# One kernel, three edits: the order of the two heads in probabilities-by-values, a transposed copy of the input from the host, and a contiguous layout for the compression operand

## The chip, the core and the metric

The program runs on one core of a Trainium2 chip. The metric is the device time of one execution in microseconds (us). TensorE (PE) does the matrix products, VectorE (DVE) and ScalarE (ACT) the elementwise work, GpSimd (POOL) a little of it, and SyncE (SP) issues most of the DMAs. PSUM is the memory that PE writes to, SBUF the one that it reads from.

## The reference, cut to what matters

One sequence of 512 tokens, 1024 wide, goes through four blocks. The parts that the change touches are these:

```
first block, layer 0:  gated delta rule (GDN)
    proj = x @ w_in                # x is the kernel's input; 4096 columns for q, k, v, z, and 16 for a and b
first block, layer 1:  native sparse attention (NSA)
    kc, vc = compress_blocks(...)  # 31 blocks of 32 tokens, one every 16 tokens:
        blk = x[:, 16*n + (0..31)] + pos          # n = 0..30
        silu(blk.reshape(31, 32*64) @ w1) @ w2
    per head: o = gate * (softmax(q k^T + bias) @ v), for the selected and the window branch
second block, two layers: per head, softmax(q k^T) @ v in the MLA branch and in the chunked branch
```

After each attention and GDN layer of the first block comes a mixture of experts (MoE), which the change leaves alone.

## The kernel before, in words

All operands of the large products are fp32 numbers split into two parts, hi and lo. `Net.split` (lines 107 and 108) copies the rounded value on ACT (line 107) and subtracts it on DVE (line 108). `Net.mm3` (lines 112 to 114) then makes three products, hi*hi, hi*lo and lo*hi, into the same PSUM tile. The activations that such a product needs stand in a pair `xh`, `xl` of eight tiles of 128 features by 512 tokens.

Weights come as chunks of 128x1024 (512 KB) through a ring of four SBUF buffers called `raw` (`Net.chunk`, DMA at line 96 on SP's queue). A buffer is free again when its chunk is split.

The kernel is written in a framework that puts the instructions of each engine in order before the run, by its own model of when each would be ready, with earlier work in program order first. An engine then runs its queue strictly in that order. A PE instruction whose operand is not ready holds back all that is behind it. Where the model saw a gap in front of an instruction, it has put a later one there that was ready.

**Start.** SP's queue loads the constants `call` (line 78), then the input `x` in four chunks of 128 tokens (line 1753, in `tile_network`), then small things of `gdn`: `row`, `nw`, `cw`, `wab` (lines 242 to 270). Each chunk of `x` is transposed on PE in eight pieces (`to_xt`, line 187) into PSUM and split from there. `wab` holds the 16 columns for a and b. It is split (`wabh`, `wabl`), and 24 products of `mm3` with 16 output rows follow, into a PSUM tile `br`. Then comes the projection of k with the first chunk of `g_w`.

**Compression.** `nsa` projects the keys and values to be compressed and stores them in `X0` and `X1`, tiles of 128x5x512. Partitions 0 to 63 hold the features of token t, partitions 64 to 127 those of token t+1, so that one product takes two of a block's 32 tokens. `x_evac` fills them from PSUM (lines 130 and 132, 16 copies of 64 partitions by 512 or 511). `compress` (line 1210) then makes 16 products for each of k and v. The moving operand is `Xs[i][:, :, l:l + 481:16]`: five groups (four heads and the position embedding) of 31 elements, 16 elements apart, 155 columns in all.

**Probabilities by values.** `softmax_t` works on one head: for each of four query tiles scores, a maximum with the bias (line 1142), the exponential (1144), its scaling on DVE (1147 or 1149), transposes on PE (187), and copies to `PT` on ACT (1151). Two heads u = 0 and 1 share a PSUM tile `o`, head 0 in partitions 0 to 63 and head 1 in 64 to 127, so each product uses half of PE's columns. The products (line 1333 in `nsa`, line 1613 in `pv_pair` of the second block) run over four key tiles jt, with 512, 384, 256 and 128 columns, and within each over u = 0, 1. Each fp32 product stands as two instructions in the trace, so a pair of heads has 16. There are 16 such pairs in NSA (four groups, two pairs of heads, two branches) and 16 in the second block (two layers, two branches, four pairs).

Around them stand products that are ready early and have no other hurry: the queries of the next group in NSA, and the gate and branch projections (PSUM tile `br`) in the second block.

Of the kernel before, what the change touches and what calls it, by code (L numbers as in the profile page):

```python
# [19 lines left out]
T = 512  # L20
# [45 lines left out]
class Net:  # L66
    def __init__(self, ctx, tc, I, out, dbg):
        self.tc, self.nc, self.I, self.out, self.dbg = tc, tc.nc, I, out, dbg
        self.cst = ctx.enter_context(tc.tile_pool(name="cst", bufs=1))
        self.ring = ctx.enter_context(tc.tile_pool(name="ring", bufs=1))  # L70
        self.big = ctx.enter_context(tc.tile_pool(name="big", bufs=1))
        self.lnp = ctx.enter_context(tc.tile_pool(name="lnp", bufs=1))
        self.ps, self.banks, self.pool = None, {}, ExitStack()
        self.dr = ctx.enter_context(tc.tile_pool(name="dr", bufs=1, space=bass.MemoryType.DRAM))
        nc = self.nc
        names, arr = _consts()
        call = self.cst.tile([128, arr.shape[1]], F32, name="call")
        nc.sync.dma_start(call, I["cst"])
        self.c = {n: call[:, j * 128:(j + 1) * 128] for j, n in enumerate(names)}
        self.ident = self.c["ident"]  # L80
        self.pows = self.cst.tile([128, 32], F32, name="pows")
        nc.vector.memset(self.pows, -0.5)
        self.flip = self.turn = self.turn2 = 0
        self.more, self.pairs = [], []


    def dump(self, name, ap):
# [140 lines left out]

def gdn(net, xt, aside):

# [4 lines left out]
    with ExitStack() as cx:  # L235
# [28 lines left out]
        with ExitStack() as c1:  # L264
# [3 lines left out]
            nc.sync.dma_start(cw, I["g_cw"])  # L268
            wab = p1.tile([128, 128], F32, name="wab")
            nc.sync.dma_start(wab, I["g_ab"])  # L270
            wabh = p1.tile([128, 128], F32R, name="wabh")
            wabl = p1.tile([128, 128], F32R, name="wabl")
            net.split(wabh, wabl, wab)
            XN = p1.tile([128, 32, 64], F32, name="XN")
# [806 lines left out]
def _prep_nsa(i, a):  # L1081
# [14 lines left out]
    a["n_w2"] = np.concatenate([w2[0], w2[0], w2[1]], 1)  # L1096
    a["n_pos"] = np.concatenate(ps, 1)
    a["n_rel"] = i["rel_bias"].T
# [61 lines left out]
def nsa(net, xt):  # L1160
# [4 lines left out]
    with ExitStack() as cx:  # L1165
# [11 lines left out]
        with ExitStack() as c1:  # L1177
# [10 lines left out]
            for i in range(2):  # L1188
                X = p1.tile([128, 5, T], F32, name=f"X{i}")
                G.memset(X[:, 4], 0.0)  # L1190
                G.memset(X[64:128, :, T - 1:], 0.0)
                G.dma_start(X[:, 4, 0:32], I["n_pos"][:, i * 32:i * 32 + 32])
                Xs.append(X)
            def x_evac(m, ps):
                X = Xs[m // 2]
                for j in range(2):
                    s = slice(j * 64, j * 64 + 64)
                    net.copy(X[0:64, 2 * (m % 2) + j], ps[s])
                    net.copy(X[64:128, 2 * (m % 2) + j, :T - 1], ps[s, 1:])
            net.proj_t([w[j] for j in range(4)], xh, xl, x_evac)  # L1200

            def compress(i):
                hp = net.psum()
                hv = hp[:, :155].rearrange("p (g n) -> p g n", n=31)
                for c in range(2):
                    raw = net.ring.tile([128, RING], F32, name="raw", tag="raw", bufs=RAW)
                    nc.sync.dma_start(raw, I["n_w1"][2 * i + c])
                    for k in range(8):
                        l = 2 * (c * 8 + k)
                        PE.matmul(hv, lhsT=raw[:, k * 128:k * 128 + 128], rhs=Xs[i][:, :, l:l + 481:16],  # L1210
                                  start=l == 0, stop=l == 30)
                hb = p1.tile([128, 2], F32, name="hb", tag="hb", bufs=2)
# [41 lines left out]
        with ExitStack() as c2:  # L1254
# [17 lines left out]
            for g in range(4):  # L1272
# [41 lines left out]
                for pr in range(2):  # L1314
# [5 lines left out]
                    for br in range(2):  # L1320
# [10 lines left out]
                        for jt in range(NT):  # L1331
                            for u in range(2):
                                PE.matmul(o[u * 64:u * 64 + 64, jt * 128:],  # L1333
                                          lhsT=vv[:, jt, br * 256 + g * 64:br * 256 + g * 64 + 64],
                                          rhs=pt_rhs(PTs[u], jt), start=False, stop=br == 1 and jt == NT - 1)
# [53 lines left out]
class Second:  # L1389
# [27 lines left out]
    def run(self, done, aside=lambda: None):  # L1417
# [6 lines left out]
        with ExitStack() as cx:  # L1424
# [180 lines left out]
            with ExitStack() as c2:  # L1605
                ap = c2.enter_context(tc.tile_pool(name="att", bufs=1))

                def pv_pair(PTs, vt, p, i, yf):
                    o = net.psum()
                    for jt in range(NT):  # L1610
                        for u_ in range(2):
                            h = 2 * p + u_
                            PE.matmul(o[u_ * 64:u_ * 64 + 64, jt * 128:], lhsT=vt[:, jt, h * 64:h * 64 + 64],  # L1613
                                      rhs=pt_rhs(PTs[u_], jt), start=jt == 0, stop=jt == NT - 1)
# [118 lines left out]
def tile_network(ctx: ExitStack, tc: tile.TileContext, I, out, dbg=()):  # L1733
# [16 lines left out]
    net.phase(mm=4, tp=2, br=2)  # L1750
    for t in range(NT):
        xx = net.ring.tile([128, RING], F32, name="raw", tag="raw", bufs=RAW)
        nc.sync.dma_start(xx, tiles(x)(t))
        net.to_xt(xx, t, *xt, tag="mm")
    moe_setup(net)
    y = gdn(net, xt, lambda room: bias_setup(net, room))
    xt = []

# [24 lines left out]
def _arrays(inputs):  # L1783
    i = {k: np.asarray(v) for k, v in inputs.items()}
    a = {"x": i["x"][0], "cst": _consts()[1], "cm": _consts_moe(), "cb": _consts_bf(), "rope": _rope_tables()}
    for prep in (_prep_gdn, _prep_moe, _prep_nsa, _prep_second):
# [18 lines left out]
```

## Time and profile before

| what | us |
|---|---|
| median of 3 runs | 2218.19 (2217.37 to 2220.05) |
| the profiled execution's own time | 2215.26 |
| span of the profile, first to last instruction | 2213.5 |
| PE busy in the span | 2114.8 (96%) |
| PE weight loads busy | 1683.9 (76%) |
| DVE busy | 1436.8 (65%) |
| ACT busy | 1122.9 (51%) |
| POOL busy | 363.0 (16%) |

Busy time of PE is from the start of an instruction to its modelled end. Back-to-back matmuls overlap, so the distance from one start to the next tells what one costs. A timeline row that stands for n instructions alike gives the time from the first's start to the last's end. In brackets stands how long the engine had been idle before, and what released it.

### The profile page before, as it was taken

The page shows a single profiled execution, that of the slowest core. Times are in us where ns is not written, and L with a number is a line of the kernel's source. Part 1 is how long each engine was busy: PE and PEld are TensorE (multiplying, and loading weights), DVE is VectorE, ACT ScalarE, POOL GpSimd, SP SyncE. Part 2 cuts the span into 40 slices and gives each one's busy share as a digit, 9 for nine tenths or more (in the row PEclk, how much of TensorE's full clock was granted, in tenths as well). Part 3 has the DMA queues.
Part 4 walks back from the last instruction along what each step waited for, and adds up shares of the span by engine and source line. Part 5 has one row for each costly group of instructions (what it writes and reads, how often), then busy time and mean ns, then how long its engine had stood idle before and what let it go on. Part 6 is the DMA issues. An engine that isn't in the chain of part 4 may idle for free.

```text
span 2213.5 us, 30328 instructions
## 1 busy us (share of the span) xinstructions
PE 2114.8 (96%) x10689; PEld 1683.9 (76%) x10689; DVE 1436.8 (65%) x2902; ACT 1122.9 (51%) x2238; POOL 363.0 (16%) x367
## 2 busy tenths in 40 slices
PE   8998988999999989899989999999999999999998
PEld 6777876877877656688778877787877887777786
DVE  6787666899538876689965554554456556455544
ACT  4545542987337776298743334544344324445432
POOL 4411013553100001355320010000011001000000
PEclk9999997999999999799999999999999999999999
DMA  6344536998441102699856555333435646433442
GB/s 205 95 133 122 163 132 241 338 329 281 139 123 49 48 29 94 232 355 334 286 161 199 157 154 156 119 105 136 150 110 171 205 134 176 133 114 110 143 152 76
DMA packets 133805, 364.86 MB, mean 165 GB/s; under 512 B 28544, under 2 KB 41296, under 8 KB 131856
## 3 DMA queue, kind: packets, MB, share of 16 engines
q1 hardware_dynamic: 80448, 271.65, 36.8%
q0 software_dynamic: 19744, 54.62, 7.9%
q10 hardware_dynamic: 33456, 36.59, 5.5%
q8 instruction: 86, 1.41, 0.3%
q14 instruction: 71, 0.58, 0.1%
HBM read 314.17 MB, written 64.61 MB: 171 GB/s over the span
## 4 chain that ended last, share of the span: by engine, by line
PE 65%; DVE 5%; DMA 5%; issue 4%; ACT 3%; POOL 1%; DVEq 0%; POOLq 0%; ACTq 0%; SPq 0%
PE mm L112 10%; PE mm L114 10%; PE mm L113 9%; PE br L113 6%; PE br L112 6%; PE br L114 5%; PE tp L187 5%; PE mm L966 5%; PE mm L1333 2%; PE mm L1613 2%; DMA xh<-in_m_w_dram 2%; DMA raw<-in_m_w_dram 1%; ACT hi L107 1%; DVE lo L108 1%; PE mm L1327 1%
## 5 line engine op out<-in xcount | busy, mean ns | idle before, releaser
L108 DVE TENSOR_TENSOR lo<-raw,hi 128x1024 fp32r<-128x1024 f32 x266 | 339.1, 1278 | 305.5 <-ACT hi L107 303.6
L107 ACT CAST hi<-raw 128x1024 fp32r<-128x1024 f32 x276 | 288.5, 1047 | 431.3 <-PE br L113 149.8
L112 PE MATMUL mm<-xh,hi 128*128 128x512 f32 x688 | 273.1, 397 | 1.7 <-DVE acc L316 1.7
L113 PE MATMUL mm<-xl,hi 128*128 128x512 f32 x688 | 271.1, 394 | 0.0
L114 PE MATMUL mm<-xh,lo 128*128 128x512 f32 x688 | 270.5, 394 | 0.1
L112 PE MATMUL mm<-hi,xh 128*128 128x512 f32 (+1 forms) x480 | 189.3, 394 | 4.9 <-ACT xh L107 4.1
L114 PE MATMUL mm<-hi,xl 128*128 128x512 f32 (+1 forms) x480 | 188.7, 394 | 1.1 <-DVE xl L108 1.0
L113 PE MATMUL mm<-lo,xh 128*128 128x512 f32 (+1 forms) x480 | 188.0, 392 | 0.0
L112 PE MATMUL br<-xh,hi 128*128 128x512 f32 x464 | 184.7, 398 | 2.2 <-DVE tm L1598 1.9
L113 PE MATMUL br<-xl,hi 128*128 128x512 f32 x464 | 186.6, 402 | 0.0
L114 PE MATMUL br<-xh,lo 128*128 128x512 f32 x464 | 182.7, 394 | 0.0
L1144 ACT ACTIVATE s<-s,mx 128x128 f32<-128x128 f32 (+3 forms) x256 | 143.1, 561 | 21.5 <-DVE mx L1142 20.8
L112 PEld LDWEIGHTS mm<-xh,hi 128*128 128x128 f32 x688 | 130.9, 190 | 29.6 <-issue 2.4
L114 PEld LDWEIGHTS mm<-xh,lo 128*128 128x128 f32 x688 | 130.1, 189 | 28.3 <-DVE lo L108 1.2
L113 PEld LDWEIGHTS mm<-xl,hi 128*128 128x128 f32 x688 | 130.8, 190 | 26.8
L1151 ACT COPY PT<-tp 128x128 f32<-128x128 f32 (+3 forms) x256 | 103.0, 425 | 30.8 <-PE tp L187 29.7
L112 PEld LDWEIGHTS mm<-hi,xh 128*128 128x128 f32 x480 | 91.5, 191 | 24.7 <-ACT xh L107 5.6
L966 PE MATMUL mm<-hi,xeh 128*128 128x512 f32 x256 | 109.8, 429 | 0.0
L187 PE MATMUL tp<-call,s 128*128 128x128 f32 x640 | 107.8, 278 | 0.8 <-ACT PT L1151 0.4
L114 PEld LDWEIGHTS mm<-hi,xl 128*128 128x128 f32 x480 | 91.4, 190 | 21.1 <-DVE xl L108 3.2
L187 PEld LDWEIGHTS tp<-call,s 128*128 128x128 f32 x640 | 74.9, 140 | 41.6 <-ACT PT L1151 17.1
L113 PEld LDWEIGHTS mm<-lo,xh 128*128 128x128 f32 x480 | 91.4, 190 | 17.5 <-issue 0.2
(514 smaller groups left out, 4562.9 us busy)
## 6 DMA issues: line engine op xcount, KB each, us to landing
raw<-in_s_w_dram SPq DMA_DIRECT2D x128, 512.0 KB, 3.6
raw<-in_m_w_dram SPq DMA_DIRECT2D x48, 512.0 KB, 10.4
xh<-in_m_w_dram SPq DMA_DIRECT2D x44, 512.0 KB, 11.8
raw<-in_g_w_dram SPq DMA_DIRECT2D x40, 512.0 KB, 3.7
xl<-in_m_w_dram SPq DMA_DIRECT2D x40, 512.0 KB, 12.8
raw<-in_n_w_dram SPq DMA_DIRECT2D x32, 512.0 KB, 3.8
ho<-in_m_w_dram SPq DMA_DIRECT2D x24, 512.0 KB, 9.2
raw<-in_s_br_dram SPq DMA_DIRECT2D x24, 512.0 KB, 3.5
```

Of the source, the lines that this page charges most:

```text
L107: self.nc.scalar.copy(hi, src)
L108: (eng or self.nc.vector).tensor_tensor(lo, src, hi.bitcast(F32), op=OP.subtract)
L112: mm(ps, lhsT=ah, rhs=bh, start=start, stop=False)
L113: mm(ps, lhsT=ah, rhs=bl, start=False, stop=False)
L114: mm(ps, lhsT=al, rhs=bh, start=False, stop=stop)
L187: self.nc.tensor.transpose(tp[:, j], src(b + j), self.ident)
L966: PE.matmul(pg, lhsT=a[:, c * 2 + k], rhs=b[:, k * 512:k * 512 + 512], start=c + j == 0, stop=c == 3 and j == 5)
L1144: S.activation(p[:, :n], s[:, :n], AF.Exp, bias=mx, scale=-1.0, accum_out=sm)
L1151: S.copy(PT[:, t:4 * t + 1:3], tp)
L1327: PE.matmul(ps[:, :n], lhsT=qs[j][:, ts], rhs=kh[:, :n], start=True, stop=False)
L1333: PE.matmul(o[u * 64:u * 64 + 64, jt * 128:], lhsT=vv[:, jt, br * 256 + g * 64:br * 256 + g * 64 + 64], rhs=pt_rhs(PTs[u], jt), start=Fals ...
L1613: PE.matmul(o[u_ * 64:u_ * 64 + 64, jt * 128:], lhsT=vt[:, jt, h * 64:h * 64 + 64], rhs=pt_rhs(PTs[u_], jt), start=jt == 0, stop=jt == NT - 1)
```

## The change

Three edits.

1. The loop over the two heads in probabilities by values runs u = 1 first, then u = 0, at both places.
2. The host passes a second copy of the input, transposed (`xT`, eight pieces of 128 features by 512 tokens). The kernel loads two pieces at a time into a ring buffer and splits them straight into `xh`, `xl`; the transposes of `x` go. `wab` is loaded first of all, through a ring buffer, and split at once into a tile that shares its memory with a later one (tag `pg`). The constants are loaded after the input.
3. `X0` and `X1` become 128x5x8x32: element (k, n) is token 16n + 2k on partitions 0 to 63, and token 16n + 2k + 1 on 64 to 127. The copies out of PSUM take every second token into that order, 256 elements each, and the moving operand of a product is 31 elements side by side. The host lays out the position embedding alike, padded with zeros, and the memsets of `X` go.

```diff
@@ Net.__init__, Net.consts
-        nc.sync.dma_start(call, I["cst"])
+    def consts(self):
+        self.nc.sync.dma_start(self.call, self.I["cst"])
@@ new function
+def gdn_small(net):
+    ab = net.lnp.tile([128, D], F32R, name="pg", tag="pg", bufs=1)
+    wabh, wabl = ab[:, 0:128], ab[:, 128:256]
+    wab = net.ring.tile([128, RING], F32, name="raw", tag="raw", bufs=RAW)[:, :128]
+    net.nc.sync.dma_start(wab, net.I["g_ab"])
+    net.split(wabh, wabl, wab)
+    return wabh, wabl
@@ gdn
-            wab = p1.tile([128, 128], F32, name="wab")
-            nc.sync.dma_start(wab, I["g_ab"])
-            wabh = p1.tile([128, 128], F32R, name="wabh")
-            wabl = p1.tile([128, 128], F32R, name="wabl")
-            net.split(wabh, wabl, wab)
@@ _prep_nsa (host)
-    a["n_pos"] = np.concatenate(ps, 1)
+    ps = np.concatenate(ps, 1).reshape(128, 2, 2, 8, 2)[..., 0].transpose(0, 1, 3, 2)
+    a["n_pos"] = np.concatenate([ps, np.zeros((128, 2, 8, 30), ps.dtype)], 3).reshape(128, 512)
@@ nsa
-                X = p1.tile([128, 5, T], F32, name=f"X{i}")
-                G.memset(X[:, 4], 0.0)
-                G.memset(X[64:128, :, T - 1:], 0.0)
-                G.dma_start(X[:, 4, 0:32], I["n_pos"][:, i * 32:i * 32 + 32])
+                X = p1.tile([128, 5, 8, 32], F32, name=f"X{i}")
+                G.dma_start(X[:, 4].rearrange("p r n -> p (r n)"), I["n_pos"][:, i * 256:i * 256 + 256])
@@ x_evac
-                    s = slice(j * 64, j * 64 + 64)
-                    net.copy(X[0:64, 2 * (m % 2) + j], ps[s])
-                    net.copy(X[64:128, 2 * (m % 2) + j, :T - 1], ps[s, 1:])
+                    v = ps[j * 64:j * 64 + 64].rearrange("p (n r u) -> p u r n", r=8, u=2)
+                    for u in range(2):
+                        net.copy(X[u * 64:u * 64 + 64, 2 * (m % 2) + j], v[:, u])
@@ compress
-                        l = 2 * (c * 8 + k)
-                        PE.matmul(hv, lhsT=raw[:, k * 128:k * 128 + 128], rhs=Xs[i][:, :, l:l + 481:16],
-                                  start=l == 0, stop=l == 30)
+                        PE.matmul(hv, lhsT=raw[:, k * 128:k * 128 + 128], rhs=Xs[i][:, :, k, c:c + 31],
+                                  start=c + k == 0, stop=c == 1 and k == 7)
@@ nsa, line 1332, and pv_pair, line 1611
-                            for u in range(2):
+                            for u in (1, 0):
@@ tile_network
-    for t in range(NT):
+    g_small = gdn_small(net)
+    for j in range(4):
         xx = net.ring.tile([128, RING], F32, name="raw", tag="raw", bufs=RAW)
-        nc.sync.dma_start(xx, tiles(x)(t))
-        net.to_xt(xx, t, *xt, tag="mm")
+        for u in range(2):
+            nc.sync.dma_start(xx[:, u * T:u * T + T], I["xT"][2 * j + u])
+        v = xx.rearrange("p (k t) -> p k t", k=2)
+        net.split(xt[0][:, 2 * j:2 * j + 2], xt[1][:, 2 * j:2 * j + 2], v)
+    net.consts()
```

## Rows read from the trace of the kernel before

**Rows 1.** The page's part 4: the last chain, share of the span by engine.
```profile
PE 65%; DVE 5%; DMA 5%; issue 4%; ACT 3%; POOL 1%; DVEq 0%; POOLq 0%; ACTq 0%; SPq 0%
```

**Rows 2.** Busy time by stretch: PE, PEld, DVE, ACT, POOL; granted clock, DMA share, GB/s.
```profile
560.00:660.00 100.00, 98.71 (x461) 77.94 (x460) 42.97 (x77) 34.92 (x56) 8.73 (x16) 1.00 0.40 128
...
676.00:722.00 46.00, 45.93 (x260) 32.56 (x258) 39.26 (x149) 35.37 (x106) 0.00 (x0) 1.00 0.14 45
...
1310.00:1424.00 114.00, 113.83 (x565) 88.17 (x566) 58.09 (x169) 54.90 (x130) 0.46 (x4) 1.00 0.54 160
```

**Rows 3.** Timeline of the start: start, duration, engine, line, operation, count.
```profile
4.98 5.71 PE L187 MATMUL mm<-call,raw 128*128 128x128 f32 x32 [4.98 <-DMA raw<-in_x_dram]
...
6.95 4.09 SPq L96 DMA_DIRECT2D raw<-in_g_w_dram  x4
...
12.22 0.30 ACT L107 CAST wabh<-wab 128x128 fp32r<-128x128 f32 x1 [0.74 <-DMA wab<-in_g_ab_dram]
...
12.57 0.40 PE L112 MATMUL br<-xh,wabh 128*16 128x512 f32 x1 [1.89 <-ACT wabh L107]
...
13.43 1.05 ACT L107 CAST hi<-raw 128x1024 fp32r<-128x1024 f32 x1 [0.92 <-DMA raw<-in_g_w_dram]
...
14.51 3.72 DVE L108 TENSOR_TENSOR lo<-raw,hi 128x1024 fp32r<-128x1024 f32 x3 [1.61 <-ACT hi L107]
...
18.13 0.40 PE L112 MATMUL mm<-xh,hi 128*128 128x512 f32 x1
...
18.64 0.69 SPq L96 DMA_DIRECT2D pg<-in_m_w_dram  x1
```

**Rows 4.** Timeline of PE, the two compressions.
```profile
611.40 8.59 PE L1210 MATMUL mm<-X,raw 128*128 128x155 f32 x32
...
630.72 8.59 PE L1210 MATMUL mm<-X,raw 128*128 128x155 f32 x32
```

**Rows 5.** Timeline of PE in GDN: fp32 products with a contiguous moving operand.
```profile
301.23 1.06 PE L556 MATMUL mm<-vp,XT 128*128 128x128 f32 x8
```

**Rows 6.** Line 130's copies into X: count, then ns minimum, median, maximum.
```profile
L130 ACT COPY X<-mm x8: 581/583/586, 587.1 to 603.6; 64x512 f32<-64x512 f32 x8
```

**Rows 7.** Timeline of PE in the second block, MLA branch, and at its end.
```profile
1335.22 1.07 PE L1613 MATMUL mm<-PT,vt 128*64 128x512 f32 x2
1336.23 0.98 PE L187 MATMUL tp<-call,s 128*128 128x128 f32 x7
1336.96 0.48 PE L112 MATMUL br<-xh,hi 128*128 128x512 f32 x1
...
1338.08 2.37 PE L1613 MATMUL mm<-PT,vt 128*64 128x512 f32 x14
1340.37 0.50 PE L113 MATMUL br<-xl,hi 128*128 128x512 f32 x1
...
2077.24 1.07 PE L1613 MATMUL mm<-PT,vt 128*64 128x512 f32 x2
```

**Rows 8.** Timeline of PE in the second block, chunked branch.
```profile
1434.00 2.37 PE L1613 MATMUL mm<-PT,vt 128*64 128x512 f32 x16
1436.31 0.50 PE L112 MATMUL br<-xh,hi 128*128 128x512 f32 x1
```

**Rows 9.** Timeline of DVE beside the split at 1335.22.
```profile
1335.67 0.49 DVE L1147 TENSOR_SCALAR s<-s,sm 128x512 f32<-128x512 f32 x1
```

**Rows 10.** Timeline of all engines in NSA, the first pair.
```profile
681.80 1.07 PE L1333 MATMUL mm<-PT,vv 128*64 128x512 f32 x2
...
682.24 0.55 DVE L1149 TENSOR_SCALAR s<-s,sm,gt 128x512 f32<-128x512 f32 x1
...
682.81 0.55 PE L187 MATMUL tp<-call,s 128*128 128x128 f32 x3
```

**Rows 11.** Timeline of PE in NSA, between two groups of heads.
```profile
822.20 1.09 PE L187 MATMUL tp<-call,pc 128*128 128x128 f32 x4 [4.88 <-DVE pc L1310]
```

**Rows 12.** Busy time in that stretch, columns as in rows 2.
```profile
821.20:827.90 6.70, 5.03 (x14) 3.52 (x15) 1.89 (x7) 1.59 (x5) 0.00 (x0) 0.50 0.00 0
```

More of the change, by code (lines that the diff above doesn't have):

```diff
@@ L76, in __init__ @@
         names, arr = _consts()
-        call = self.cst.tile([128, arr.shape[1]], F32, name="call")
-        nc.sync.dma_start(call, I["cst"])
-        self.c = {n: call[:, j * 128:(j + 1) * 128] for j, n in enumerate(names)}
+        self.call = self.cst.tile([128, arr.shape[1]], F32, name="call")
+        self.c = {n: self.call[:, j * 128:(j + 1) * 128] for j, n in enumerate(names)}
         self.ident = self.c["ident"]
@@ L226, in rows, with gdn @@
         return r
-def gdn(net, xt, aside):
+def gdn_small(net):
[5 more added lines that the diff above has]
+    return wabh, wabl
+def gdn(net, xt, aside, wabh, wabl):
     tc, nc, I = net.tc, net.nc, net.I
@@ L1610, in pv_pair @@
                     for jt in range(NT):
-                        for u_ in range(2):
+                        for u_ in (1, 0):
                             h = 2 * p + u_
@@ L1750, in tile_network @@
     net.phase(mm=4, tp=2, br=2)
-    for t in range(NT):
+    g_small = gdn_small(net)
+    for j in range(4):
         xx = net.ring.tile([128, RING], F32, name="raw", tag="raw", bufs=RAW)
-        nc.sync.dma_start(xx, tiles(x)(t))
-        net.to_xt(xx, t, *xt, tag="mm")
+        for u in range(2):
[3 more added lines that the diff above has]
+    net.consts()
     moe_setup(net)
-    y = gdn(net, xt, lambda room: bias_setup(net, room))
+    y = gdn(net, xt, lambda room: bias_setup(net, room), *g_small)
     xt = []
@@ L1784, in _arrays @@
     i = {k: np.asarray(v) for k, v in inputs.items()}
-    a = {"x": i["x"][0], "cst": _consts()[1], "cm": _consts_moe(), "cb": _consts_bf(), "rope": _rope_tables()}
+    a = {"x": i["x"][0], "xT": i["x"][0].T.reshape(8, 128, T), "cst": _consts()[1], "cm": _consts_moe(), "cb": _consts_bf(), "rope": _rope_tables()}
     for prep in (_prep_gdn, _prep_moe, _prep_nsa, _prep_second):
```

## The prediction

> **What bounds the kernel now.** I read the last chain first: 65% of the span is PE's, no other engine has more than 5% [rows 1]. Then the stretches that the change touches. In 560 to 660 us (keys, values, compression) PE is busy 98.7 of 100 us, in an MLA stretch 113.8 of 114; DVE and ACT are at about half there or less. In NSA PE is busy 45.9 of 46 us as well, but DVE 39.3 and ACT 35.4 [rows 2]. So PE's time is the kernel's time in the first two, and in NSA nearly so: there DVE is close behind, and a busy PE need not be a PE that could not have waited. The reader is to ask of each edit how many us of PE's queue go, and whether another wait stands right behind them. Last I read the timeline at each place.
>
> **Edit 1, second head first.** A pair of heads has 16 product instructions. In 26 of the 32 pairs (16 in NSA, ten in the second block, the last at 2077.24) they stand split: two instructions, head 0's first key tile, ahead of the last transposes of head 1, and 14 after those [rows 7, 10]. In the other six all 16 stand together [rows 8]. From the first product's start to the next operation's, 16 together take 1436.31 - 1434.00 = 2.31 us [rows 8], the 14 take 1340.37 - 1338.08 = 2.29 us [rows 7]. The two split off are then free if they come with the others (the two heads use different halves of PE's columns, and run side by side), and cost 1336.23 - 1335.22 = 1.01 us alone [rows 7], plus some 0.1 us of a longer step into them: 1.1 us of PE's queue.
>
> With head 1 first, nothing of the pair is ready before head 1's last copy. Head 0's products were all ready at the time of the split, and yet only the one that is first in program order was brought forward; so the order within a pair is kept, and I expect 16 together everywhere. On PE's queue 26 x 1.1 = 28.6 us go.
>
> What is late next? The split products were put where PE would have stood. At 1336.23 PE goes on with seven transposes, and their operand is scaled by DVE from 1335.67 to 1336.16 [rows 7, 9]: left as it is, PE would have waited till then anyhow, and 0.07 us would be won. In NSA at 682.81 the same: DVE's scaling ends at 682.79 [rows 10]. I set each of the 26 against the last scaling and the last copy that ended before PE's next operation: with all other work in its place 11.5 us are won, 3.9 in the second block and 7.6 in NSA. That is the lower bound; 28.6 is the upper.
>
> Between them it is a matter of filler. In the second block the gate projection has operands ready (it goes on at 1336.96 with a chunk split long before [rows 7]), DVE and ACT are half idle, and a matmul moved into the gap takes it. So PE's sum decides there: I take 9.5 of 10 x 1.1 = 11 us. In NSA there are queries of the next group as filler for half the pairs of the first three groups, and the softmax of the next pair only as far as its buffers reach; DVE is at 85%. I take the middle between 7.6 and 17.6, a little to the low side as the row at 682.81 is the commoner kind: 10.5. Sum 20 us.
>
> **Edit 3, the compression operand.** Its 32 instructions take 8.59 us, twice [rows 4]. Less one latency of some 0.43, one comes every (8.59 - 0.43) / 31 = 0.263 us. Products of the same kind on 128 contiguous columns come every (1.06 - 0.27) / 7 = 0.113 us [rows 5], the weights being just as large; for 155 columns that scales to 0.113 x 155 / 128 = 0.137, less its fixed part some 0.134. The one difference is the step of 16 elements. Contiguous, each saves 0.13 us, 64 instructions 8.3 us. The other end is nothing, if it is not the step but the five short groups. I take 8.3: the nearest row speaks for it, and PE is busy throughout [rows 2].
>
> The copies into `X` get shorter but read PSUM with a step. Now ACT's take 0.58 us for 512 columns [rows 6]; for 256 I would say 0.3 to 0.4, and if the step cost them fourfold, 1.5. They are eight for a pair of PSUM tiles, in turn on ACT and DVE, one after the other; the pair after the next needs the banks 48 matmuls later, at (18.13 - 12.57) / 24 = 0.23 us each [rows 3] 11 us. Even 8 x 1.2 us would be covered; fourfold would be late by a us or two a pair, 4 us in all. The memsets that go are on POOL, which nobody waits for here.
>
> The Trainium skill (SBUF - State Buffer, section "Door 1: The DMA port swizzle") says that SBUF is read in lines of 16 bytes, that fp32 may step by 4 elements at no cost and pays beyond, and that PSUM's lines have 8 bytes, so that a non-contiguous pattern there slows matmuls. Its first half is the gain, and the row at 0.263 agrees. Its second half speaks against the new copies, if it holds for reads by ACT and DVE too; no run here shows one. By the rule at its worst the sum loses those 4 us.
>
> **Edit 2, the start.** Before, PE's 32 transposes take it from 4.98 to 10.69; it then waits for `wab`, which is last of all in SP's queue and split at 12.22, does the 24 products for a and b, and begins the k projection at 18.13 [rows 3]. After, `wab` comes first, and the input needs four splits, 1.05 us on ACT and 3.72 / 3 = 1.24 on DVE [rows 3]. The first piece of `x` has less ahead of it in the queue than now, so it is there by 4.98 at the latest; its lo is made by 4.98 + 1.05 + 1.24 = 7.3, the fourth's by about 7.3 + 3 x 1.24 = 11. The last six products then end at 12.4 at best. PE starts slowly now: 32 transposes in 5.71 us, 0.18 each, against (0.98 - 0.27) / 6 = 0.12 later [rows 3, 7]. If the 24 products all ran at half pace, 0.46 us, from 6 on, they would end at 17.
>
> But the k projection needs the first chunk of `g_w`. Its DMA waits for a ring buffer, now free at 6.95, after at 7.3, and as many bytes lie ahead of it as before; so it lands at about 13.4 again, hi is ready at 14.5, lo at 14.51 + 1.24 = 15.75 [rows 3]. The third matmul of the projection needs lo: at 15.75 instead of 18.13 + 0.46 = 18.59. That is 2.8 us, and PE has 24 matmuls (5.5 us) for each chunk from there on, while chunks come every 1.24 us, so the gain is kept. Bounds: 1 us (half pace to the end) and 18.13 - 12.4 = 5.7 (the chunk lands early).
>
> Moved past the input are only the constants: they are needed by the small transposes behind the 24 products, not before 12.4, and the transfer that is now last had landed at 12.2 [rows 3]; late, they would cost a few tenths. The tile in which `wab` now lives takes an MoE weight chunk at 18.64 in the old order [rows 3]. That load must wait for the 24 products, which end sooner than 18.13, and its user comes hundreds of us later: nothing. Should SP's queue stand for it, the ring's next loads behind it have a chunk's 5.5 us of margin.
>
> **Sum.** 20 + 8.3 + 2.8 = 31 us off 2215.3, the profiled execution's own time: 2184. The median of the runs lies 2.9 us above that execution, so 2187. A new order of the queues can shift other waits by some us either way; I have no row for that.
>
> **The rivals.**
> - A, the gaps stay: the pairs come together, but PE waits where the split was. Edit 1 gives its lower bound: 11.5 + 8.3 + 2.8 = 22.6, so 2195.6. For it: the scalings that end at 682.79 and 1336.16 [rows 9, 10]. Against it: the filler seen at 1336.96 [rows 7].
> - B, all of it and more: edit 1 at 28.6, the start at 4: 41, so 2177. For it: PE near 100% in both stages [rows 2]. Against: DVE at 85% in NSA.
> - C, the step is not what costs: edit 3 gives nothing, or the copies eat it; 23 us, 2195. Against it: a factor of two between rows 4 and 5.
> - D, the change does not do what it says: the split stays in another shape, head 0's product brought forward alone. Then 11 us, 2207. Against it: only the first in program order was ever brought forward.
> - E, slower: the split products are what keeps PE going in NSA. Where PE had waited 4.88 us for DVE [rows 11], the granted clock stood at 0.50 (1.2 GHz instead of 2.4) for 6.7 us [rows 12], which costs up to 3.4 us. If the emptied gaps brought such falls, nine would eat the 31 us, and from eleven on it is slower by more than 0.2%: 2187 + 11 x 3.4 = 2224; all 26 places would give 2275. Against it: the gaps are a us at most, a fifth of the wait before the fall shown.
>
> **How the numbers follow.** The forecast 0.58 (2179 to 2193 by its own terms), A 0.2, B 0.1, C 0.04, D 0.03, E 0.05. The range takes A, B and C and leaves out D and E and the edge of B: 2172 to 2205. What a measurement of this kernel can tell from no change is about 0.2%, 4.4 us. All but E lie beyond it on the fast side; for E and for a new order that undoes much of it, I give slower 0.05, same 0.03, faster 0.92.
>
> **What would show it.** Edit 1: lines 1333 and 1613 stand in runs of 16, 32 of them, of 2.3 us, and the MLA stretch of 114 us is some 4 us shorter; in NSA the same products are followed by waits that now are not seen. Edit 3: line 1210's 32 instructions take 4.3 to 4.7 us. Edit 2: no transposes at the start, the third matmul of the k projection at about 15.8. Wrong would be: runs of two still there; 8 us still for line 1210; waits of PE for line 1147 or 1149 as long as the products that went; a clock at 0.50 in NSA more often than now.

## The result, and the profile of the changed kernel

| | before | changed |
|---|---|---|
| median of the runs | 2219.12 us (2217.37 to 2220.70, 4 runs) | 2187.36 us (2186.32 to 2188.46, 4 runs) |
| ratio, 95% interval | | 0.9857 (0.984 to 0.9874) |
| profiled execution / its span | 2215.26 / 2213.5 us | 2186.32 / 2184.6 us |
| mean granted clock | 0.978 | 0.974 |

The changed kernel is 31.8 us faster by the medians, 28.9 us in the profiled executions. The forecast was 2187.0 us, 31 us less. The total is as predicted; its parts are not, and the rest of this document is about that. The profiled execution of the kernel before is a fast one (2215.26 us, below all four runs of this table), that of the changed kernel is 1.0 us below its median; what follows compares profiles, and so starts from the 28.9.

Line numbers shift: split is now L109 and L110, `mm3` L114 to L116, the transposes L189, the compression L1216, the products of probabilities by values L1339 and L1619.

The two compressions, which answer to [rows 4], in the timeline of PE (start, duration, engine, line, operation, count):

```profile
611.45 4.37 PE L1216 MATMUL mm<-X,raw 128*128 128x155 f32 x32
...
626.59 4.37 PE L1216 MATMUL mm<-X,raw 128*128 128x155 f32 x32
```

8.59 us each before, 4.37 now. The copies that feed them, answering to [rows 6] (count, then ns minimum, median, maximum):

```profile
L132 ACT COPY X<-mm x8: 365/368/371, 587.2 to 603.4; 64x256 f32<-64x256 f32 x8
```
```profile
L134 DVE COPY X<-mm x8: 417/423/427, 587.6 to 603.8; 64x256 f32<-64x256 f32 x8
```

The products of probabilities by values, answering to [rows 7, 8, 10], timeline of PE in NSA and in the second block:

```profile
677.14 2.37 PE L1339 MATMUL mm<-PT,vv 128*64 128x512 f32 x16
685.98 2.37 PE L1339 MATMUL mm<-PT,vv 128*64 128x512 f32 x16
...
1303.06 2.37 PE L1619 MATMUL mm<-PT,vt 128*64 128x512 f32 x16
1318.15 2.37 PE L1619 MATMUL mm<-PT,vt 128*64 128x512 f32 x16
```

All 32 pairs stand as 16; from the first start to the next operation 31 of them take 2.30 us (one is followed by a wait). No two-and-fourteen is left.

The start, answering to [rows 3], timeline of ACT, DVE and PE:

```profile
6.61 0.61 PE L114 MATMUL br<-xh,pg 128*16 128x512 f32 x1 [6.61 <-ACT xh L109]
...
12.11 0.63 PE L116 MATMUL br<-xh,pg 128*16 128x512 f32 x1
...
12.54 0.63 PE L114 MATMUL br<-xh,pg 128*16 128x512 f32 x1
...
12.64 1.05 ACT L109 CAST hi<-raw 128x1024 fp32r<-128x1024 f32 x1 [1.21 <-DMA raw<-in_g_w_dram]
...
15.50 0.40 PE L116 MATMUL br<-xh,pg 128*16 128x512 f32 x1
15.93 0.68 DVE L291 COPY abs__174<-br 16x512 f32<-16x512 f32 x1 [3.29 <-PE br L116]
...
16.66 0.42 PE L294 MATMUL tp<-call,abs__174 16*128 16x16 f32 x4 [0.77 <-DVE abs__174 L291]
17.01 0.50 PE L114 MATMUL mm<-xh,hi 128*128 128x512 f32 x1
...
17.23 1.22 DVE L110 TENSOR_TENSOR lo<-raw,hi 128x1024 fp32r<-128x1024 f32 x1
...
18.50 0.50 PE L116 MATMUL mm<-xh,lo 128*128 128x512 f32 x1 [0.27 <-DVE lo L110]
```

The third matmul of the k projection in program order, the first that needs the low half of the weights, stands at 18.50; before it was 18.60, the forecast was 15.8. (In PE's queue it is now the fifth: two more that need no low half were put ahead of it.) The chunk came early: its high half was ready at 12.64 + 1.05 = 13.69. But DVE stood idle for 3.29 us, from 12.64 to 15.93, because the next instruction in its queue was the copy of the a/b product (L291), which had to wait for the last of the 24 products at 15.50. The low half was behind that copy.

**Where the time went, stage by stage.** For each stage, how much longer or shorter it is than in the profile of the kernel before, in us. It is worked out from the start times of the same product in both traces (first compression product at 611.40 before; then the products that stand at 641, 912 and 1200 before; then the end of the span). The last column is the stretch at clock 0.50 early in the MoE of layer 1.

```
                              start   comp-    NSA     MoE 1   second    sum    clock 0.50
                             to 611  ression  to 912  to 1200   block            near 900
changed kernel                +0.1    -8.4    -15.8    +6.0    -10.8   -28.9    30.7
changed kernel, again         -0.8    -8.4    -15.8    +7.6    -10.2   -27.6    30.7
edit 1 alone                  +3.7     0.0    -15.9    +3.8    -10.7   -19.1    27.3
edit 2 alone                  -0.9     0.0      0.0    +1.6     +1.8    +2.5    23.9
edit 3 alone                  -1.0    -8.4     +0.1    +0.9     +0.2    -8.2    23.9
edits 1 and 3                 -1.4    -8.4    -15.6    +2.2    -11.1   -34.4    20.5
edits 1 and 3, again          +3.2    -8.4    -16.4    +3.8    -11.2   -29.0    23.9
changed, start reordered      -3.0    -8.4    -15.5    +5.7     -9.8   -31.1    27.3
before, other steps (1)       +0.9    -3.5     -0.1    +3.5     +1.4    +2.2    27.3
before, other steps (2)       +2.0    -4.7     +0.2    +4.0     +0.4    +1.9    27.3
predicted                     -2.8    -8.3    -10.5     0       -9.5   -31.1
```

The two rows of other steps are the kernels of the last experiment below; they have none of the three edits.

The columns of compression, NSA and second block hardly differ between kernels with the same edits. The first column does, even among kernels that begin alike: the seven profiles with the old start reach the compression at 609.97 to 615.11 us (median 612.28). A gain of 2.8 us at the start can't be read from one profile. The four with the new start as changed reach it at 610.50 to 611.45; whether some of the lead is left there, these numbers can't tell.

### The profile page after: what moved, and what is told of

It is laid out like the page before. It is cut to its first block, busy times and chain, and to the rows that moved or that the text cites. A ratio compares the mean times of both kernels' runs of the same rounds, so it can differ in the third digit from the quotient of the medians.

```text
span 2184.6 us, 30258 instructions
## 1 busy us (share of the span) xinstructions
PE 2081.1 (95%) x10657; PEld 1662.7 (76%) x10657; DVE 1427.6 (65%) x2898; ACT 1118.6 (51%) x2234; POOL 367.6 (17%) x363
## 4 chain that ended last, share of the span: by engine, by line
PE 45%; DMA 4%; DVE 4%; issue 3%; ACT 1%; POOL 1%; DVEq 0%; POOLq 0%; SPq 0%; ACTq 0%
PE mm L114 8%; PE mm L116 7%; PE mm L115 7%; PE br L114 5%; PE br L116 5%; PE br L115 5%; PE tp L189 2%; DMA raw<-in_m_w_dram 2%; PE mm L1619 2%; PE mm L973 2%; DMA xh<-in_m_w_dram 1%; DVE lo L110 1%; DMA xl<-in_m_w_dram 1%; ACT hi L109 1%; DMA qk<-qkd 1%
## 5 line engine op out<-in xcount | busy, mean ns | idle before, releaser
L110 DVE TENSOR_TENSOR lo<-raw,hi 128x1024 fp32r<-128x1024 f32 x266 | 338.5, 1276 | 297.3 <-ACT hi L109 294.6
L109 ACT CAST hi<-raw 128x1024 fp32r<-128x1024 f32 x276 | 288.5, 1047 | 418.3 <-PE mm L115 146.2
L114 PE MATMUL mm<-xh,hi 128*128 128x512 f32 x688 | 273.1, 397 | 2.1 <-DVE acc L323 2.1
L116 PE MATMUL mm<-xh,lo 128*128 128x512 f32 x688 | 270.5, 394 | 0.4 <-DVE lo L110 0.3
L114 PE MATMUL mm<-hi,xh 128*128 128x512 f32 (+1 forms) x480 | 189.2, 394 | 4.9 <-ACT xh L109 4.2
L116 PE MATMUL mm<-hi,xl 128*128 128x512 f32 (+1 forms) x480 | 188.5, 393 | 1.6 <-DVE xl L110 1.5
L114 PE MATMUL br<-xh,hi 128*128 128x512 f32 x464 | 186.0, 401 | 2.2 <-DVE tm L1604 1.9
L116 PE MATMUL br<-xh,lo 128*128 128x512 f32 x464 | 184.4, 398 | 0.0
L114 PEld LDWEIGHTS mm<-xh,hi 128*128 128x128 f32 x688 | 130.9, 190 | 29.6 <-issue 2.8
L116 PEld LDWEIGHTS mm<-xh,lo 128*128 128x128 f32 x688 | 130.4, 190 | 29.2 <-DVE lo L110 2.0
L114 PEld LDWEIGHTS mm<-hi,xh 128*128 128x128 f32 x480 | 91.3, 190 | 24.6 <-ACT xh L109 5.6
L189 PE MATMUL tp<-call,s 128*128 128x128 f32 x640 | 107.3, 277 | 2.0 <-ACT PT L1160 0.9
L116 PEld LDWEIGHTS mm<-hi,xl 128*128 128x128 f32 x480 | 91.3, 190 | 21.5 <-DVE xl L110 3.8
L115 PEld LDWEIGHTS mm<-lo,xh 128*128 128x128 f32 x480 | 91.3, 190 | 17.6 <-issue 0.2
L114 PEld LDWEIGHTS br<-xh,hi 128*128 128x128 f32 x464 | 87.8, 189 | 21.2 <-issue 3.2
## 6 DMA issues: line engine op xcount, KB each, us to landing
raw<-in_m_w_dram SPq DMA_DIRECT2D x48, 512.0 KB, 11.2
```

Of the source, the lines that this page charges most:

```text
L109: self.nc.scalar.copy(hi, src)
L110: (eng or self.nc.vector).tensor_tensor(lo, src, hi.bitcast(F32), op=OP.subtract)
L114: mm(ps, lhsT=ah, rhs=bh, start=start, stop=False)
L115: mm(ps, lhsT=ah, rhs=bl, start=False, stop=False)
L116: mm(ps, lhsT=al, rhs=bh, start=False, stop=stop)
L189: self.nc.tensor.transpose(tp[:, j], src(b + j), self.ident)
```

## The experiments

**Each edit by itself.** Three kernels, the kernel before with one edit each, and one with two.

```diff
e1_order:  -  for u in range(2):      +  for u in (1, 0):      # both places, nothing else
e2_start:  transposed input, wab first, constants last, nothing else
e3_comp:   X as 128x5x8x32, contiguous moving operand, nothing else
e13:       e1_order and e3_comp together, the start as before
```

> The kernel before with the second head first in both PV places, nothing else. Theory from the two traces: NSA stage 15.8 us shorter and second block 12.0 us shorter, with 0 to 6 us given back in the MoE stages: 2219 less 22 to 28, 2191 to 2197. The prediction's own terms (10.5 and 9.5) say 2199. Rival: the gain of the changed kernel's NSA stage came from the compression standing earlier and not from the order: then NSA gives 8 to 11 and the time is 2198 or more. In the trace all 32 pairs stand as 16 together of 2.30 us.

> The kernel before with the transposed input and the early a/b operand alone. Theory: the k projection's third matmul waits for VectorE, whose low half of the first weight chunk is queued behind the copy of the a/b product; it stands at 18.5 as before (18.59), and the time is within 1 us of before, 2218 to 2220. The prediction's term says 2216.4 (2.8 less), with that matmul at 15.8. Rival: the start gains and the clock gives it back: third matmul at 16 to 17, and a fall of the granted clock at about 235 us that the kernel before hasn't got.

> The kernel before with the compression operand stored by pair alone. Both the prediction and the comparison of the traces say 8.3 to 8.4 us less: 2210.8. The 32 matmuls of one compression take 4.37 us, 0.131 apart. Rival: the gain stays behind in the NSA stage, whose softmax work then waits for something else: 2213 to 2219.

> Edits 1 and 3 together with the old start. If the start gives nothing, this is the time of the changed kernel, 2187 within 1.5 us; if the new start costs by its clock (the fall at 235 us), 2183 to 2185; if the prediction's 2.8 us are in the changed kernel after all, 2190.

Measured, beside 19 runs of the kernel before (median 2219.85 us): edit 1 2196.17 us (ratio 0.9886, 0.9872 to 0.9901), edit 2 2220.43 (1.001, 1.0001 to 1.002), edit 3 2212.37 (0.9967, 0.9954 to 0.9981), edits 1 and 3 2181.98 (0.983, 0.9817 to 0.9844).

So edit 1 gave 23.7 us, some 3 us more than by the prediction's terms (2199) and inside the theory's 2191 to 2197. Its NSA stage is 15.9 us shorter without the new compression, so the rival for NSA falls. Edit 3 gave 7.5 us by the medians and 8.4 in its own stage, and nothing of it was given back in NSA (its rival). Edit 2 gave nothing; if anything it cost 0.2 to 4 us. The first product that needs the low half stands at 17.85 there, 0.7 us earlier than before and not 2.8, and the copy is ahead of the low half again. The rival's fall of the clock near 235 us is not in this profile. Timeline of DVE and PE in the kernel with edit 2 alone:

```profile
15.28 0.68 DVE L291 COPY abs__174<-br 16x512 f32<-16x512 f32 x1 [2.92 <-PE br L116]
...
16.58 1.22 DVE L110 TENSOR_TENSOR lo<-raw,hi 128x1024 fp32r<-128x1024 f32 x1
...
17.85 0.50 PE L116 MATMUL mm<-xh,lo 128*128 128x512 f32 x1 [0.29 <-DVE lo L110]
```

Edits 1 and 3 without edit 2 came out below all three numbers that were expected, nearest to the one by which the new start costs. The fall near 235 us, on which that number rested, does not go with the new start: the changed kernel has it in one profile (235.3 us) and not in its second, and the second profile of edits 1 and 3, with the old start, has one at 236.4. Whether the new start costs was to be seen with both kernels on one chip.

**The changed kernel again, without edit 2, and with the start reordered.** The third kernel forces two orders: on DVE the low half of the first chunk ahead of the copy of a/b, on PE the first chunk's products ahead of the a/b transposes.

```diff
 fix, in gdn (the a/b tail is traced from the k projection's first evacuation)
+                with tc.issue_after(net.los[n_lo].ins):        # the first chunk's lo
                     V.tensor_copy(abs_, ab[:16])
+                with tc.issue_after(net.mms[n_mm + 7].ins):    # its eighth group of products
                     for t in range(NT):
                         PE.transpose(tp[:, t, :16], ...)
```

> The changed kernel once more, beside the next two on one chip. Theory (the 6.1 us that it lost in the first MoE layer are a longer stretch of granted clock 0.50, 30.7 us against 23.9): if that stretch comes out shorter this time, its profile is shorter by about half of what the stretch lost, and the MoE stage gives back 2 us instead of 6. If it is the order of the instructions, the same 6 us are lost at the same places. Time 2185 to 2189.

> Edits 1 and 3 with the old start, once more, beside the changed kernel. If the new start costs, as 2182.0 against 2187.4 said, it is faster again by 3 to 6 us; if those were two chips, the two agree within 1.5 us.

> The changed kernel with two orders forced at the start: VectorE makes the low half of the first weight chunk before it copies the a/b product, and TensorE does the first chunk of the k projection before the small a/b transposes. Theory (queue order is what kept the start late): the low half is there at 15.0, the third matmul of the k projection at about 16.2 instead of 18.50, 2.3 us earlier, and the later stages follow until the clock moves them. Rival: something else is late next (the second chunk's low half, the gate values g that the k heads need), the lead is gone by 45 us. Time 2183 to 2188 by what the clock makes of it.

Measured, beside 9 runs of the kernel before (median 2219.97 us): the changed kernel 2186.6 us (0.9847, 0.9834 to 0.986), edits 1 and 3 2183.94 (0.9838, 0.9825 to 0.9852), the reordered start 2184.2 (0.9838, 0.9825 to 0.9852). Without edit 2 the kernel is 2.7 us faster here, between the two answers that were expected, and was 5.4 us faster by the medians of the first two comparisons; the intervals overlap here, so it is no slower, and more can't be said. Edits 1 and 3, and the reordered start, have the lowest medians of the study, and their intervals are the same.

The reordering did what it was to do. Timeline of DVE and PE with the reordered start (line numbers are one to seven higher here):

```profile
13.53 1.23 DVE L111 TENSOR_TENSOR lo<-raw,hi 128x1024 fp32r<-128x1024 f32 x1 [1.07 <-ACT hi L110]
...
15.71 0.40 PE L115 MATMUL mm<-xh,hi 128*128 128x512 f32 x1
...
15.91 0.68 DVE L298 COPY abs__238<-br 16x512 f32<-16x512 f32 x1 [1.16 <-PE br L117]
...
16.63 0.40 PE L117 MATMUL mm<-xh,lo 128*128 128x512 f32 x1
```

The low half is there at 13.53 + 1.23 = 14.76, PE goes from a/b straight into the k projection at 15.71, and the first product with the low half stands at 16.63 instead of 18.50 (the fifth product here too). So the order of the queues made the wait that took the place of the one removed: this is shown, for DVE's and PE's orders together. The lead does not last: against the kernel before, the same products stand 2.2 us earlier at 45 us, 2.7 later at 64, 0.3 earlier at 95, 3.1 earlier at 237. Between 54 and 64 us the trace shows why: at 57.11 PE stands 2.96 us for DVE's `A` (L370), a wait that the kernel before hasn't got at this place, and right behind it, from 57.7 to 61.1, the granted clock is 0.50. So the rival, that something else is late next, holds for that stretch; what delayed `A`, and what gave the lead back by 237, was not followed further.

The expectation for the second run of the changed kernel did not decide: its stretch at clock 0.50 near 900 was again 30.7 us, and the MoE lost again. The comparison across kernels, below, speaks for the clock in part of it.

**How much running alone costs.** The loops over heads and key tiles are exchanged, so that one head's eight records stand together.

```diff
-                        for jt in range(NT):
-                            for u in (1, 0):
+                        for u in (1, 0):
+                            for jt in range(NT):
```

> The changed kernel with the loops over heads and key tiles exchanged in both PV places: head 1's eight records, then head 0's, so that no two of different heads stand next to each other. Theory (the split cost 1.0 us because two records of one head ran alone, where in pairs they run side by side on two halves of the columns): one head's eight records take 2 x 0.48 x (1 + 0.75 + 0.5 + 0.25) = 2.4 us, a pair 4.8 to 4.9 instead of 2.30, the kernel 32 x 2.5 = 81 us slower, 2265 to 2270. Rival (the 1.0 us was the step in and out of the products, not running alone): a pair takes 2.3 to 2.9, the kernel 2187 to 2206.

Measured: 2234.23 us (one run), 47.6 more than the changed kernel's 2186.6. Timeline of PE at the first pair (compare 677.14 above):

```profile
676.84 3.93 PE L1339 MATMUL mm<-PT,vv 128*64 128x512 f32 x16
680.69 0.77 PE L189 MATMUL tp<-call,s 128*128 128x128 f32 x5
```

A pair takes 680.69 - 676.84 = 3.85 us and not 2.30: 1.55 more, and 32 x 1.55 = 50 us. The rival (2.3 to 2.9) falls, but so does the size of the theory (4.8). The starts of the records say why. The first four of head 1 (512 and 384 columns, two each) start 0.48, 0.43, 0.32 and 0.32 us apart, alone. Its fifth starts at 678.389 and head 0's first at 678.395: from there on head 1's short half runs beside head 0's long half. Only what finds no partner is paid. The two split records of the kernel before had none, which is their 0.48 + 0.52 = 1.0 us [rows 7].

**Which step of the operand costs.** The kernel before, with its compression reading the same tile with other steps.

```diff
-  rhs=Xs[i][:, :, l:l + 481:16]
+  rhs=Xs[i][:, :, l:l + 30 * STEPS[i][c] + 1:STEPS[i][c]]
+STEPS = ((1, 2), (4, 8))      # steps
+STEPS = ((4, 3), (2, 1))      # steps2
```

> The kernel before; its compression reads the same operand with other steps: k's first 16 instructions with step 1 and its next 16 with step 2, v's first 16 with step 4 and its next 16 with step 8, instead of 16 (the compressed keys and values are then other sums). Theory A (the cost is there once neighbouring elements of a read no longer share a line of 16 bytes; the Trainium skill, SBUF - State Buffer, section Door 1: The DMA port swizzle, has it so for TensorE's reads): steps 1, 2 and 4 run at 0.13 us an instruction, step 8 at 0.26 as step 16. Theory B (the cost grows with the step): 0.13, then in between, then 0.26. Theory C (it was the five short groups and not the step): 0.26 at every step. In the changed kernel it is 0.131 at step 1 and in the kernel before 0.263 at step 16.

> As the run before, with the steps changed about: k's instructions with 4 and then 3, v's with 2 and then 1 (again other sums). In the run before an instruction came every 0.134 us at step 1, 0.142 at 2, 0.276 at 4, 0.280 at 8. Theory (the step sets it, and the read is full speed as long as two elements share a line of 16 bytes): k's at step 4 0.28 and v's at steps 2 and 1 0.14 and 0.13; at step 3, where a line holds one or two elements, in between, 0.18 to 0.23. Rival (it was v's operand or its place, not the step): v's stay at 0.28 and k's at 0.13 to 0.14.

These two kernels compute other sums; only the spacing is read from them. Busy time of this line alone in stretches of 16 products each, from the start of the first to a little past the start of the last (PE busy and count, PEld, granted clock, DMA share, GB/s). Steps 1, 2, 4 and 8, in this order:

```profile
612.28:614.43 2.15, 2.15 (x16) 2.15 (x16) 1.00 0.03 13
614.43:616.72 2.29, 2.29 (x18) 2.17 (x16) 1.00 0.24 75
627.62:632.04 4.42, 4.42 (x16) 3.31 (x16) 1.00 0.25 49
632.04:636.50 4.46, 4.46 (x17) 3.12 (x15) 1.00 0.64 190
```

Steps 4, 3, 2 and 1 in the second kernel:

```profile
613.36:617.78 4.42, 4.42 (x16) 3.31 (x16) 1.00 0.01 2
617.78:621.13 3.35, 3.35 (x17) 2.97 (x15) 1.00 0.53 157
632.07:634.34 2.27, 2.27 (x17) 2.27 (x17) 1.00 0.01 4
634.34:636.49 2.15, 2.15 (x18) 2.06 (x16) 1.00 0.42 122
```

A sixteenth of each is the time from start to start: 0.134 us at step 1, 0.142 at 2, 0.209 at 3, 0.276 at 4, 0.279 at 8. At 16 it was 0.263 [rows 4]. It is the step, whichever operand has it, and not the five short groups (theory C). The whole price is there at step 4, and nothing is added beyond. So a step of up to 2 is nearly free and theory A was wrong at 4. The Trainium skill (SBUF - State Buffer, section "Door 1: The DMA port swizzle") states two things of SBUF reads in general: at least two hits in a line of 16 bytes are needed for full speed, and fp32 may step by 4 for free. The runs bear out the first (step 2, at 0.142 us, still has two elements in such a line) and contradict the second (0.276 us at step 4).

## Why the prediction was right, and where it was not

**Edit 3: right.** 0.134 us an instruction was forecast, (4.37 - 0.29) / 31 = 0.132 was measured, 0.29 being the last one's duration. The stage is 8.4 us shorter in every kernel with this edit, against 8.3. The copies cost 0.37 us on ACT, as estimated, and 0.42 on DVE. That is what contiguous copies let one expect: 0.20 and 0.22 us for 64 elements and 0.58 and 0.68 for 512 (`vcb` and `vv`, same lines) put 256, on a straight line, at 0.37 and 0.42. So the step cost nothing that can be seen, and what the prediction had feared from PSUM's lines did not come.

**Edit 1: right in its mechanism, too small in its NSA term.** The pairs came together everywhere, at 2.30 us, and the gain is PE's queue. NSA was put at 10.5 us and gave 15.5 to 16.4; the second block was put at 9.5 and gave 9.8 to 11.2 (with the little that follows it). The step that failed is the one called "the middle between 7.6 and 17.6". The groups of PE in the NSA stage show it (line, operation, tile, count; busy us, mean ns; idle time before, with its releasers), first of the kernel before, 641 to 868 us:

```profile
L1333 PE MATMUL mm<-PT,vv 128*64 128x512 f32 (+3 forms) x256 | 55.0, 442 | 0.3 <-ACT PT L1151 0.2
L187 PE MATMUL tp<-call,s 128*128 128x128 f32 x320 | 53.0, 280 | 0.7 <-ACT PT L1151 0.4
L1327 PE MATMUL mm<-kh,qst 128*128 128x256 f32 (+2 forms) x128 | 48.6, 388 | 1.4 <-DVE mx L1142 1.1
...
L1318 PE MATMUL mm<-pcT,vcb 128*128 128x512 f32 x16 | 9.6, 686 | 1.8 <-ACT pcT L1313 1.7
L1293 PE MATMUL mm<-qst,kph 128*128 128x512 f32 x16 | 7.0, 440 | 0.8 <-DVE qst L1266 0.7
```

and of the kernel with edit 1 alone, 644 to 856 us (same line numbers; two records of L1333 fall outside the stretch):

```profile
L187 PE MATMUL tp<-call,s 128*128 128x128 f32 x320 | 51.9, 278 | 1.8 <-ACT PT L1151 0.8 <-DVE s L1149 0.6
L1327 PE MATMUL mm<-kh,qst 128*128 128x256 f32 (+2 forms) x128 | 49.7, 393 | 1.8 <-DVE mx L1142 1.6
...
L1333 PE MATMUL mm<-PT,vv 128*64 128x512 f32 (+3 forms) x254 | 37.9, 440 | 0.4
...
L1318 PE MATMUL mm<-pcT,vcb 128*128 128x512 f32 x16 | 9.5, 680 | 2.0 <-ACT pcT L1313 2.0
L1293 PE MATMUL mm<-qst,kph 128*128 128x512 f32 x16 | 6.9, 433 | 0.8 <-DVE qst L1266 0.7
```

The products fall from 55.0 to 37.9 us of busy time, which runs to modelled ends and so holds overlap with what comes next. From start to start a split pair took 1.01 + 2.29 us [rows 7] and one together takes 2.30, so a split cost 1.0 us and not 1.1, 16.0 in the stage. The waits ahead of these five groups rise, from 0.3 + 0.7 + 1.4 + 1.8 + 0.8 = 5.0 us to 1.8 + 1.8 + 0.4 + 2.0 + 0.8 = 6.8 us. But PE's longest wait in the stage, the one between two groups of heads [rows 11], shrinks by more than that (in total, times, longest; the kernel before, then edit 1 alone):

```profile
PE tp L187 <- DVE pc L1310: 5.1, 2, 4.9
```
```profile
PE tp L187 <- DVE pc L1310: 2.8, 2, 2.2
```

All of PE's idle time from the last compression product to the last of these products is 10.2 us before and 9.6 with edit 1; it is 9.8 to 10.2 in the five profiles with the old order and 9.5 to 9.8 in the six with the pairs together. So nothing of what went came back as waiting, and the stage is 228.66 - 213.45 = 15.2 us shorter, nearly the whole 16.0. The lower bound had set each split against the scaling that ended just before PE's next operation, with all else in its place. But the framework orders the queue anew, and the gaps were filled. Rival A, by which the waits would have grown by the better part of what went, falls with this. The second block's term was of the right size.

**Edit 2: wrong.** The step that failed is the wait for the low half: "hi is ready at 14.5, lo at 14.51 + 1.24 = 15.75". The high half was ready sooner, at 13.69. The low half was made at 17.23, because on DVE it stood behind the copy of the a/b product and a small sum (L291, L297), and on PE the k projection stood behind four small transposes. I had counted DMAs and PE, and had not written down DVE's queue, though the rows show every engine running strictly in its order. The reordered start shows the wait and takes it away: 18.50 becomes 16.63.

A second thing holds the start back even then. The 32 transposes that edit 2 took off PE had run at half pace at first, and PE had come to full pace with nothing else done. Stretches of the start, columns as in [rows 2], of the kernel before (transposes, transposes, a/b products):

```profile
4.98:8.70 3.72, 3.72 (x18) 3.63 (x19) 1.66 (x3) 1.80 (x4) 2.15 (x3) 1.00 0.97 386
8.80:10.69 1.89, 1.88 (x16) 1.43 (x14) 1.73 (x4) 1.89 (x5) 1.28 (x11) 1.00 0.33 89
12.57:18.13 5.56, 5.56 (x24) 2.39 (x25) 3.91 (x5) 3.15 (x3) 3.30 (x12) 1.00 1.02 342
```

and of the changed kernel (a/b products, slow and then fast):

```profile
6.60:13.39 6.79, 6.13 (x14) 1.94 (x15) 4.95 (x5) 3.99 (x5) 4.25 (x15) 1.00 0.98 356
13.43:15.73 2.30, 2.30 (x11) 0.85 (x9) 0.00 (x0) 0.26 (x1) 2.30 (x20) 1.00 0.94 338
```

(The clock column says 1.00 since there is no record before the first rise, at 8.77 us before and 13.43 after; the spacing shows the pace.) Before, transposes stood 3.72 / 18 = 0.21 us apart, then 0.12, and the a/b products found PE at full pace, 5.56 / 24 = 0.23 apart. In the changed kernel these products, the first thing PE does, are 0.43 apart (12.54 - 12.11) up to 13.4. Fourteen of them at 0.2 us more are 2.8 us, and their last stands at 15.50. The prediction had this as a bound ("half pace to the end", 17). The other profiles agree: in the seven with the old start the first record of 1.00 lies between 8.4 and 13.7 us, each time before the a/b products begin; in the five with the new start it lies between 12.4 and 13.5, in the midst of them. So work removed at the start was in part work that PE's slow first microseconds would have taken anyway; no run put other work in its place. The Trainium skill (TensorE: Matmul & The Clock Gate, section "Part 4: PE-mode transpose") says that full rate does not engage for PE's transpose mode. Here it did at 8.77 us, when PE had done nothing but the kernel's transposes; no row names their mode.

**Not in the prediction: 6 us lost in the MoE of layer 1.** Here the granted clock fell to 0.50 (1.2 of 2.4 GHz) for longer. Stretches at 0.50, of the kernel before:

```profile
916.70:940.60 23.90, 12.87 (x75) 10.90 (x75) 12.88 (x53) 3.81 (x7) 5.17 (x6) 0.50 0.77 282
```

of the changed kernel, and of the kernel with edits 1 and 3:

```profile
890.70:921.40 30.70, 18.80 (x98) 16.32 (x99) 15.74 (x56) 5.09 (x8) 6.70 (x7) 0.50 0.77 284
```
```profile
892.50:913.00 20.50, 9.37 (x62) 7.93 (x62) 11.61 (x51) 3.46 (x6) 5.17 (x6) 0.50 0.79 292
```

The code there is the same in all. From the products at 912 us to those at 950 us the ten profiles of the table lose or gain by the length of the stretch: 30.7 us +3.7 (both times), 27.3 us +1.5 to +1.9, 23.9 us -0.1 to +0.6, 20.5 us -1.5. That the length alone puts ten profiles, with and without each edit, on one line is evidence that this part is the clock and not the order of the instructions; no run set the clock, so it is not more than that. From 950 to 1200 us the kernels with edit 1 lose another 2.2 to 3.9 us, edits 2 and 3 alone 0.9 to 1.0, and the two kernels with other steps, which have no edit, 2.0 and 2.3: so it is not edit 1 that divides them. There are falls there too (1088.6 and 1112.5 us in the changed kernel, 1107.9 and 1124.9 before), of the same total length in both, 10.2 us. What this part is, is open. Over the whole stage the kernels with other steps lose 3.5 and 4.0 us against the one profile of the kernel before, so that profile may be a fast one here, and not all of the 6 us need be the edits' doing. Open is also why the stretch near 900 is longest with all three edits: both profiles of the changed kernel have 30.7 us, but the reordered start, which has all three edits too, has 27.3, and edit 2 alone 23.9.

**The sum.** Predicted 8.3 + 20 + 2.8 = 31.1. In the profiled execution: 8.4 + 15.8 + 10.8 = 35.0 from edits 3 and 1, nothing from the start, and 6.0 lost in the MoE; less a tenth at the start that makes 28.9 (2215.26 - 2186.32). The total was right because edit 1 gave 6.6 us more than forecast, while the MoE took 6.0 and the start withheld 2.8. That this comes out within 3 us of the sum is luck. So is the nearness of the medians: the forecast added 2.9 us from the profiled execution to the median, but the changed kernel's lies only 1.0 above its own. Rival E, the clock, had the right kind of price in the wrong place: in NSA there was one fall of 6.8 us, as before [rows 12].

## What to carry to other kernels

Where a move makes an operand early, write out the queue of every engine between it and its user, the elementwise engine's too: what stands ahead there takes the place of the wait removed. Where an engine's queue is its limit and independent work is at hand, removed work counts nearly in full (15.2 of 16.0 us here), and "all else in its place" is too low a bound when a scheduler orders the queue anew. Compare traces stage by stage, between the same instructions: the stages in which the edits worked repeated within 1.5 us here, while two profiles of one kernel differed by 4.6 us in a stage that no edit touched.

## What the hardware showed that was not expected

- An fp32 moving operand in SBUF costs double from a step of 4 elements on (0.276 us for 155 columns), half of that extra at 3 (0.209), next to nothing at 2 (0.142 against 0.134); 16 is no worse (0.263).
- ACT's and DVE's reads of PSUM with a step of 16 elements show no such price: 0.37 and 0.42 us for 256 elements, against 0.58 and 0.68 for 512 elements without a step (L132 and L134 into `vv`).
- Products on two halves of PE's columns overlap across the seam of two runs also: the fifth record of one head and the first of the other started 6 ns apart.
- PE's first microseconds of work ran at half pace in both kernels, on transposes in one and on products in the other; the transposes of the input had paid that for the products behind them.
